# A hybrid DiT block on one core: the first feed-forward's output product in pieces of 2 and a last piece of 4, and the mixer blocks' norm scaling on ScalarE

## The chip, the cores and the metric

The kernel runs on one core of a Trainium2 chip. The metric is the device time of one execution in microseconds, as the median of several runs. The five engines that the profile tells apart are PE (TensorE; its weight loads are listed as PEld), DVE (VectorE), ACT (ScalarE), POOL (GpSimd) and SP (SyncE, which here issues all DMAs).

## The reference, cut to what matters

Only the first feed-forward network (ffn1) and the norm ahead of the mixer are touched. In the reference they are these lines, for the 512 rows of x and, with the same weights, for the 256 rows of the context:

```python
def rmsnorm(x, g):
    y = x32 * lax.rsqrt(jnp.mean(x32 * x32, axis=-1, keepdims=True) + EPS)
    return (y * g.astype(jnp.float32)).astype(x.dtype)

def swiglu(h, w_in, w_out):
    gate, up = jnp.split(h @ w_in, 2, axis=-1)
    return (jax.nn.silu(gate) * up) @ w_out

h = ada_pre(x, norm_pre[l, 0], m[0], m[1])
x = ada_post(x, swiglu(h, ffn1_w_in[l], ffn1_w_out[l]), norm_post[l, 0], m[2], 0.5)
h = ada_pre(x, norm_pre[l, 1], m[3], m[4])
y, yc = mixer(h, hc, ...)
```

`ada_post` is z + w * gate * rmsnorm(y, g); `ada_pre` is rmsnorm(z, g) * (1 + scale) + shift. The model width is 1024 and the inner width of ffn1 2816. After the mixer comes a second feed-forward (ffn2), which the change leaves alone.

## The kernel before, in words

All 768 rows are worked on together as six blocks of 128 rows: four of x (0 to 3) and two of the context (4 and 5), taken in the order 4, 5, 0, 1, 2, 3 (`ORDER`). Every product is made from float32 values split into a high and a low part (`split`, lines 65 and 66: a cast on ACT, then a subtraction on DVE), with three matmuls in place of one (`mm3`, lines 71, 72 and 74; `product`, lines 425 to 427).

The inner width is 22 column tiles of 128. `in_tile(j)` makes one column tile of silu(gate) * up, for all 768 rows. Tiles 0 and 1 are made by the plain product (`std_tile`); meanwhile DVE and ACT form sums of the input blocks (`sums1`, `sums1_t4`), and from tile 2 on a tile is made by a scheme of seven half-size products (`product` seven times, with 12 matmuls in each), for which `weights(j)` loads the gate and the up columns (512 KB each, into the tile `wraw`, of which there are three buffers), splits the up columns (g0), adds them up in place (lines 411 to 414) and splits the results (g2, g1 and the half-size c). The high and low parts go into `wh` and `wl`, of three buffers each. The forms of the input that three of the seven products read stand in `fxh` and `fxl`. The product of form T3 (F_T3), the fifth of the seven, is the last to read `fxl`.

The output product is cut into pieces by `run_pieces`: a piece is a few column tiles whose contributions are summed in PSUM before they are taken out. For a piece, `out_w(j)` loads row block j of the output weights (512 KB, into `wraw` too) and splits it into `woh` and `wol`, of two buffers each in ffn1; the very last block goes into `wh` and `wl`. `out_phase` then runs over the six blocks of rows: six matmuls per column tile and block, two halves of 512 columns. The first piece's sums are copied out by ACT (line 332), those of the middle pieces are added to `tok` by DVE (line 334: twelve additions per piece), and those of the last piece go to `last1`. The pieces of ffn1 are (1, 2, 2, 2, 2, 2, 2, 2, 2, 2, 3). A piece's `out_phase` is written after the first `in_tile` of the next piece, so PE has one `in_tile` between a piece's tiles and its output product.

`last1` works on one block after the last piece's matmuls: the two halves are added (line 727), ACT squares the block and sums it (`rstd`, line 226), POOL makes the reciprocal root in two instructions on 128 values (lines 228 and 229), DVE multiplies by the gate (line 729) and adds the residual (line 730), for which x or the context is loaded again into `wraw` (line 736). Then `pre_xn` makes the norm for the mixer: again squares on ACT, two POOL instructions, and the scaling on DVE (line 234). When two blocks are ready, `make_hT` transposes them on PE (line 250), scales and shifts them on ACT (line 257; the first of eight on DVE, line 255), and splits them on DVE (lines 259 and 260). The mixer's first projections (`proj_tok`, and `part` of its first gate) come next on PE, by pairs of blocks: (4, 5), (0, 1), (2, 3). Their results are copied to `vt` on ACT (line 908).

What sets the order: at the very start of the kernel it is written out by hand (`manual_schedule`); everywhere else the framework orders each engine's instructions when the kernel is built, by the order of the program and the buffers that are free. An engine works through its own list in order, and waits where a value or a buffer is not ready. Parallel to ffn1, DVE computes the modulation vectors in small steps (`background`, lines 637 to 687), 1.7 steps at each `product`.

Of the kernel before, what the change touches and what calls it, by code (L numbers as in the profile page):

```python
# [11 lines left out]
F32R = mybir.dt.float32r  # L12
AF = mybir.ActivationFunctionType
# [3 lines left out]
P = 128  # L17
D = 1024
# [7 lines left out]
NF = FF // P  # L26
# [17 lines left out]
def kernel(ctx: ExitStack, tc: tile.TileContext, i, out):  # L44
    nc = tc.nc
# [5 lines left out]
    def nm(s):  # L51
        uid[0] += 1
        return f"{s}_{uid[0]}"

    def ps(tag="mm", shape=(P, 512)):
        return psum.tile(list(shape), F32, tag=tag, name=nm(tag), bufs=4)

    def ct(shape, tag, dt=F32, bufs=1, pool=None):
        return (pool or core).tile(list(shape), dt, tag=tag, name=nm(tag), bufs=bufs)
# [4 lines left out]
    def split(hi, lo, src):  # L64
        nc.scalar.copy(hi, src)  # L65
        nc.vector.tensor_tensor(out=lo, in0=src, in1=f32(hi), op=ALU.subtract)  # L66

    def mm3(outs, sh, sl, start, stop):

        for o, mh, ml in outs:  # L70
            nc.tensor.matmul(o, lhsT=sh, rhs=mh, start=start, stop=False)  # L71
            nc.tensor.matmul(o, lhsT=sh, rhs=ml, start=False, stop=False)  # L72
        for o, mh, ml in outs:
            nc.tensor.matmul(o, lhsT=sl, rhs=mh, start=False, stop=stop)  # L74

    def steps(work, n):
        while n and work:
            try:
                next(work[0])
                n -= 1  # L80
            except StopIteration:
                work.pop(0)
# [46 lines left out]
    tok = [None] * NT  # L129
# [87 lines left out]
    def rstd(z, n, scratch):  # L217

        ss = ct([P, 1], "ss", bufs=8)
        if isinstance(z, (list, tuple)):  # L220
            s2 = ct([P, 2], "ss2", bufs=4)
            for q, zz in enumerate(z):
                nc.scalar.activation(scratch[:, q * 512:(q + 1) * 512], zz, AF.Square, accum_out=s2[:, q:q + 1])
            nc.vector.tensor_tensor(out=ss, in0=s2[:, 0:1], in1=s2[:, 1:2], op=ALU.add)
        else:
            nc.scalar.activation(scratch, z, AF.Square, accum_out=ss)
        r = ct([P, 1], "rs", bufs=8)
        nc.gpsimd.tensor_scalar(ss, ss, 1.0 / n, EPS, ALU.mult, ALU.add)
        nc.gpsimd.tensor_tensor(out=r, in0=ss, in1=mhalf, op=ALU.pow)
        return r  # L230

    def pre_xn(t, xn):
        r = rstd(tok[t], D, xn)
        nc.vector.tensor_scalar(xn, tok[t], r, None, ALU.mult)
        return xn
# [60 lines left out]
    def tick(n):  # L296

        credit[0] = credit[0] + n if background else 0.0
        while background and credit[0] > 0:
            try:  # L300
                credit[0] -= next(background[0])
            except StopIteration:
                background.pop(0)

    def run_pieces(in_tile, w_out, ntok, pool, pieces, yacc, last, final_pre, order, w4, wo_bufs):
        order = order or range(ntok)

        def out_w(j):
            raw = ct([P, D], "w4", bufs=4, pool=w4) if w4 else ct([P, D], "wraw", bufs=3)
            nc.sync.dma_start(raw, w_out[j * P:(j + 1) * P, :])  # L310
            if j == NF - 1:
                hi, lo = ct([P, D], "wh", F32R, bufs=3), ct([P, D], "wl", F32R, bufs=3)
            else:
                hi = ct([P, D], "woh", F32R, bufs=wo_bufs, pool=pool)
                lo = ct([P, D], "wol", F32R, bufs=wo_bufs, pool=pool)
            split(hi, lo, raw)
            return hi, lo

        def out_phase(acts, ws, first, final):
            for t in order:  # L320
                o = [ps() for _ in range(2)]
                for hs in ((0,), (1,)) if final and t == order[-1] else ((0, 1),):
                    for q, ((ah, al), (wh, wl)) in enumerate(zip(acts, ws)):
                        mm3([(o[h], wh[:, h * 512:(h + 1) * 512], wl[:, h * 512:(h + 1) * 512]) for h in hs],
                            ah[:, t * P:(t + 1) * P], al[:, t * P:(t + 1) * P], q == 0, q == len(ws) - 1)
                if final:
                    last(t, o)
                    continue
                for h in range(2):
                    y = yacc[t][:, h * 512:(h + 1) * 512]  # L330
                    if first:
                        nc.scalar.copy(y, o[h])  # L332
                    else:
                        nc.vector.tensor_tensor(out=y, in0=y, in1=o[h], op=ALU.add)  # L334

        prev = None
        j = 0
        for n, size in enumerate(pieces):
            acts = []
            for q in range(size):  # L340
                acts.append(in_tile(j + q))
                if q == 0 and prev:
                    out_phase(*prev)
            ws = [out_w(j + q) for q in range(size)]
            prev = (acts, ws, n == 0, n == len(pieces) - 1)
            j += size
        tick(1000)
        if final_pre:
            final_pre()
        out_phase(*prev)  # L350
# [10 lines left out]
    class Forms:  # L361
# [28 lines left out]
        def last(self):  # L390
            k = 0
            for z in self.t4:
                n = z.shape[1]
                split(*self.at(F_T4, k, n), z)
                k += n
# [216 lines left out]

    GROUPS = ((0, T), (T, TA))
    HT_STEPS = {5: 8, 1: 8}
    PIECES1 = (1, 2, 2, 2, 2, 2, 2, 2, 2, 2, 3)
    PIECES = (1, 3, 3, 3, 3, 3, 2, 4)
    gg = {}

    with tc.tile_pool(name="f1", bufs=1, reuse_waits="tile") as f1:
# [93 lines left out]
        waiting = {}  # L713
# [4 lines left out]
        def post(t, o, n, v, w4, res):  # L718

            y = tok[t]  # L720
            if not scrs:
                x4 = ct([P, 4, D], "fxh", pool=w4)
                scrs.extend(x4[:, n, :] for n in range(4))
            scr = scrs[t % 4]
            for h in range(2):
                hc = slice(h * 512, (h + 1) * 512)
                nc.vector.tensor_tensor(out=y[:, hc], in0=y[:, hc], in1=o[h], op=ALU.add)
            r = rstd(y, D, ct([P, D], "up", mybir.dt.bfloat16, bufs=2, pool=w4))
            nc.vector.tensor_tensor(out=scr, in0=y, in1=gg[n, v], op=ALU.mult)
            nc.vector.scalar_tensor_tensor(out=y, in0=scr, scalar=r, in1=res, op0=ALU.mult, op1=ALU.add)  # L730
            return scr

        def last1(t, o):
            res = ct([P, D], "wraw", bufs=3)
            src = i["x"][0, t * P:(t + 1) * P, :] if t < NX else i["ctx"][0, (t - NX) * P:(t - NX + 1) * P, :]
            nc.sync.dma_start(res, src)
            scr = post(t, o, 0, 0 if t < NX else 1, f1, res)
            waiting[t] = pre_xn(t, scr)
            for s in sets:
                if t == s[-1]:  # L740
                    if not h2:
                        h2.extend(ct([P, KD, TA], tag, F32R) for tag in ("hh", "hl"))
                    hts.append(make_hT(1, *h2, s, [waiting[q] for q in s], f1, tags=("wch", "wcl")))
            steps(hts, HT_STEPS.get(t, 0))
# [4 lines left out]
        def final_pre():  # L749
            first_w.append(v_w(0))  # L750

        ffn7(i["ffn1_w_in"][0], i["ffn1_w_out"][0], forms1, NT, f1, None, PIECES1, tok, last1, pre=pre1,
             sums=(sums1, sums1_t4), acts=acts1, by_k=True, ticks=1.7, wo_bufs=2, final_pre=final_pre, order=ORDER)
        steps(hts, 1000)
# [13 lines left out]
    with tc.tile_pool(name="mh", bufs=1, reuse_waits="tile") as mh:  # L768
# [180 lines left out]
        for t in range(NX):  # L949
            o = o_tok[t // 2][:, t % 2, :]  # L950
            scr = ct([P, HG], "km", bufs=2, pool=mh)
            r = rstd(o, HG, scr)
# [188 lines left out]
    with tc.tile_pool(name="mg", bufs=1, reuse_waits="tile") as mg:  # L1141
# [44 lines left out]
        with tc.tile_pool(name="yw", bufs=1, reuse_waits="tile", side="right") as yw:  # L1186
            w2 = i["ffn2_w_in"][0]
            wout = []
            for k in range(KD):
                raw = ct([P, D], "wraw", bufs=3)  # L1190
                nc.sync.dma_start(raw, i["w_out"][0, k * P:(k + 1) * P, :])
                hi, lo = ct([P, D], "woh", F32R, bufs=4, pool=yw), ct([P, D], "wol", F32R, bufs=4, pool=yw)
# [35 lines left out]
            for t in range(NX):  # L1228
# [3 lines left out]
                r = rstd(po[t], D, ct([P, D], "junk", mybir.dt.bfloat16, pool=mg))  # L1232
# [86 lines left out]
```

## Time and profile before

| what | value |
| --- | --- |
| time, median of 3 runs | 1470.2 us (1469.75 to 1472.22) |
| the profiled execution's own time | 1468.57 us |
| its span, first to last instruction | 1466.5 us |
| busy in the span: PE, DVE, ACT, POOL | 1398.1, 1154.4, 656.9, 60.9 us |
| mean granted TensorE clock | 0.986 of full speed |

The profile gives for each engine how long it was busy and, for a group of equal instructions, the mean time of one, how long the engine stood idle just before them, and what ended that idle time. A time window can be asked for, in microseconds from the span's start. Matmuls are pipelined: one is listed with its whole passage, and the next begins before it ends, so their pace is read from the starts. ffn1's tiles fill the stretch up to about 543 us; the last piece, `last1` and the mixer's first projections follow.

### The profile page before, as it was taken

The numbers are of one execution on the slowest core, as the hardware profiler recorded it, in microseconds if no ns is written. First come the engines' busy times: TensorE is split into PE (matmuls) and PEld (weight loads), VectorE is DVE, ScalarE is ACT, GpSimd is POOL, SyncE is SP. The second block draws the span as 40 slices with busy tenths as digits, with TensorE's granted clock in tenths as the row PEclk, the third lists the DMA queues.
The fourth block names the chain that finished last, engine by engine and source line by source line (L and its number), as shares of the span: only waits on it lengthen the run. The fifth ranks groups of instructions, "written<-read, shape, count | busy, mean of one in ns | idle before, by whom it ended". The sixth has DMA issues, their size and how long they took to land. (4 is left out here: it accounts for less than half of the span.)

```text
span 1466.5 us, 22992 instructions
## 1 busy us (share of the span) xinstructions
PE 1398.1 (95%) x8864; PEld 1233.1 (84%) x8864; DVE 1154.4 (79%) x2013; ACT 656.9 (45%) x1083; POOL 60.9 (4%) x87
## 2 busy tenths in 40 slices
PE   6899999999999998999999899989898999999997
PEld 3689999999999996889888677767677998999996
DVE  6988888888888868486785789777758887787785
ACT  6553343333333335332335589523247544444442
POOL 3200000000000003000001000000010000000001
PEclk9999999999999999999999899999999999999999
DMA  9333334233333232221212121376534543343211
GB/s 312 100 115 103 113 96 120 87 91 111 90 102 96 80 101 72 83 59 45 60 42 82 41 58 30 113 203 204 170 94 142 163 134 102 99 131 101 87 44 58
DMA packets 195765, 151.61 MB, mean 103 GB/s; under 512 B 8392, under 2 KB 186056, under 8 KB 195656
## 3 DMA queue, kind: packets, MB, share of 16 engines
q1 hardware_dynamic: 195656, 150.15, 33.9%
q8 instruction: 69, 1.13, 0.3%
q14 instruction: 40, 0.33, 0.1%
HBM read 148.02 MB, written 2.10 MB: 102 GB/s over the span
## 5 line engine op out<-in xcount | busy, mean ns | idle before, releaser
L66 DVE TENSOR_TENSOR wl<-wraw,wh 128x1024 fp32r<-128x1024 f32 (+1 forms) x180 | 216.6, 1209 | 78.4 <-ACT wh L65 77.4
L65 ACT CAST wh<-wraw 128x1024 fp32r<-128x1024 f32 (+1 forms) x180 | 184.9, 1031 | 147.2 <-PE aux L426 44.7
L71 PE MATMUL mm<-hh,wh 128*128 128x512 f32 (+2 forms) x488 | 172.1, 356 | 0.3 <-ACT gg L967 0.2
L72 PE MATMUL mm<-hl,wh 128*128 128x512 f32 (+2 forms) x488 | 168.3, 353 | 0.1
L74 PE MATMUL mm<-hh,wl 128*128 128x512 f32 (+2 forms) x488 | 160.4, 359 | 3.4 <-DVE wl L66 3.4
L425 PE MATMUL mm<-hh,wh 128*128 128x256 f32 (+1 forms) x400 | 122.8, 307 | 5.3 <-DVE sg L503 5.1
L425 PE MATMUL aux<-hh,wh 128*128 128x256 f32 (+1 forms) x400 | 121.8, 304 | 2.0 <-ACT wh L65 2.0
L427 PE MATMUL aux<-hh,wl 128*128 128x256 f32 (+1 forms) x400 | 121.6, 304 | 0.0
L427 PE MATMUL mm<-hh,wl 128*128 128x256 f32 (+1 forms) x400 | 121.5, 304 | 0.0
L426 PE MATMUL aux<-hl,wh 128*128 128x256 f32 (+1 forms) x400 | 121.5, 304 | 0.0
L426 PE MATMUL mm<-hl,wh 128*128 128x256 f32 (+1 forms) x400 | 121.4, 304 | 0.0
L71 PEld LDWEIGHTS mm<-hh,wh 128*128 128x128 f32 x488 | 92.8, 191 | 14.4 <-ACT gg L967 0.7
L72 PEld LDWEIGHTS mm<-hl,wh 128*128 128x128 f32 x488 | 93.1, 191 | 10.5 <-DVE hl L557 0.6
L642 DVE SCALAR_TENSOR_TENSOR macc<-wa,cs,macc 128x256 f32<-128x256 f32 x196 | 88.0, 479 | 17.6 <-DMA wa<-w_ada 16.6
L71 PE MATMUL mm<-woh,act 128*128 128x512 f32 x252 | 98.9, 393 | 0.5 <-ACT tok L332 0.4
L74 PEld LDWEIGHTS mm<-hh,wl 128*128 128x128 f32 x488 | 89.1, 192 | 11.1 <-DVE wl L66 3.9
L72 PE MATMUL mm<-wol,act 128*128 128x512 f32 x252 | 98.1, 390 | 0.0
L334 DVE TENSOR_TENSOR tok<-tok,mm 128x512 f32<-128x512 f32 x132 | 84.5, 681 | 15.4 <-PE mm L74 15.4
L425 PEld LDWEIGHTS mm<-hh,wh 128*128 128x128 f32 x400 | 75.9, 190 | 9.1 <-DVE sg L503 7.9
L74 PE MATMUL mm<-woh,act 128*128 128x512 f32 x252 | 78.1, 390 | 0.1
L425 PEld LDWEIGHTS aux<-hh,wh 128*128 128x128 f32 x400 | 75.9, 190 | 2.5 <-ACT wh L65 2.5
L426 PEld LDWEIGHTS mm<-hl,wh 128*128 128x128 f32 x400 | 76.0, 190 | 0.6
(381 smaller groups left out, 3441.5 us busy)
## 6 DMA issues: line engine op xcount, KB each, us to landing
wraw<-ffn_w_in SPq DMA_DIRECT2D x88, 512.0 KB, 4.1
wraw<-mix_w_in SPq DMA_DIRECT2D x42, 512.0 KB, 3.7
wa<-w_ada SPq DMA_DIRECT2D x128, 128.0 KB, 2.1
b7l<-w_ada SPq DMA_DIRECT2D x96, 128.0 KB, 2.6
wraw<-ffn_w_out SPq DMA_DIRECT2D x22, 512.0 KB, 3.7
w<-ffn_w_out SPq DMA_DIRECT2D x22, 512.0 KB, 4.4
wa<-w_ada SPq DMA_DIRECT2D x16, 256.0 KB, 4.1
tok<-w_ada SPq DMA_DIRECT2D x16, 256.0 KB, 5.6
```

The lines of the kernel that those rows point to most:

```text
L65: nc.scalar.copy(hi, src)
L66: nc.vector.tensor_tensor(out=lo, in0=src, in1=f32(hi), op=ALU.subtract)
L71: nc.tensor.matmul(o, lhsT=sh, rhs=mh, start=start, stop=False)
L72: nc.tensor.matmul(o, lhsT=sh, rhs=ml, start=False, stop=False)
L74: nc.tensor.matmul(o, lhsT=sl, rhs=mh, start=False, stop=stop)
L334: nc.vector.tensor_tensor(out=y, in0=y, in1=o[h], op=ALU.add)
L425: nc.tensor.matmul(o, lhsT=wk, rhs=mh, start=first and k == 0, stop=False, skip_group_check=True)
L426: nc.tensor.matmul(o, lhsT=wk, rhs=ml, start=False, stop=False, skip_group_check=True)
L427: nc.tensor.matmul(o, lhsT=wl[:, k0 + k, :], rhs=mh, start=False, stop=k == H4 - 1, skip_group_check=True)
L642: nc.vector.scalar_tensor_tensor(out=a, in0=w, scalar=cs[:, v, k:k + 1], in1=a, op0=ALU.mult, op1=ALU.add)
```

## The change

Three edits. The pieces of ffn1 become nine of 2 tiles and a last one of 4, in place of one of 1, nine of 2 and a last one of 3. The last piece thus has four blocks of output weights at hand; `out_w(20)` is put into a new tile that takes the place of `fxl` (only in ffn1, where `w4` is None). And in `last1` the norm's scaling for the mixer is written as an activation (a copy with a scale per row) on ACT, in place of `pre_xn`, whose last step is on DVE; the squares and the POOL steps stay as they were.

```diff
             raw = ct([P, D], "w4", bufs=4, pool=w4) if w4 else ct([P, D], "wraw", bufs=3)
             nc.sync.dma_start(raw, w_out[j * P:(j + 1) * P, :])
-            if j == NF - 1:
+            if w4 is None and j == NF - 2:
+                x4 = ct([P, 4, D], "fxl", F32R, pool=pool)
+                hi, lo = x4[:, 0, :], x4[:, 1, :]
+            elif j == NF - 1:
                 hi, lo = ct([P, D], "wh", F32R, bufs=3), ct([P, D], "wl", F32R, bufs=3)
...
-    PIECES1 = (1, 2, 2, 2, 2, 2, 2, 2, 2, 2, 3)
+    PIECES1 = (2, 2, 2, 2, 2, 2, 2, 2, 2, 4)
...
             scr = post(t, o, 0, 0 if t < NX else 1, f1, res)
-            waiting[t] = pre_xn(t, scr)
+            r = rstd(tok[t], D, scr)
+            nc.scalar.activation(scr, tok[t], AF.Copy, scale=r)
+            waiting[t] = scr
```

ffn2 has pieces of its own and keeps them, and its norms keep `pre_xn`.

## Rows read from the trace of the kernel before

**Rows 1.** The page's first part: busy time, share of span, instructions.
```profile
PE 1398.1 (95%) x8864; PEld 1233.1 (84%) x8864; DVE 1154.4 (79%) x2013; ACT 656.9 (45%) x1083; POOL 60.9 (4%) x87
```

**Rows 2.** Windows: start:end, length, busy time (instructions) of PE, PEld, DVE, ACT, POOL, clock, DMA.
```profile
76.00:80.00 4.00, 3.49 (x16) 2.30 (x15) 4.00 (x5) 1.49 (x4) 0.00 (x0) 1.00 0.42 124
87.00:94.00 7.00, 7.00 (x30) 5.13 (x30) 6.97 (x12) 6.38 (x11) 0.00 (x0) 1.00 0.47 139
...
100.00:540.00 440.00, 439.02 (x2323) 409.37 (x2323) 374.18 (x634) 159.21 (x235) 0.00 (x0) 1.00 0.33 99
...
543.00:606.00 63.00, 55.25 (x306) 45.35 (x305) 46.90 (x89) 30.61 (x56) 15.81 (x24) 0.95 0.26 82
```

**Rows 3.** Windows, same columns, two short stretches inside the tail.
```profile
585.00:591.00 6.00, 5.18 (x22) 4.08 (x23) 5.68 (x15) 3.07 (x6) 2.82 (x3) 0.73 0.33 95
...
597.00:603.00 6.00, 4.44 (x26) 4.45 (x27) 2.19 (x9) 3.72 (x9) 0.00 (x0) 0.72 0.00 0
```

**Rows 4.** Waits of PE, 543 to 600 us: total, times, longest.
```profile
PE mm L71 <- ACT vt L908: 3.0, 1, 3.0
PE aux L250 <- DVE fxh L234: 2.9, 4, 1.4
```

**Rows 5.** Timeline, PE: start, us, operation; the last piece's first matmuls, its last, `proj_tok` of (2, 3).
```profile
543.21 0.39 PE L71 MATMUL mm<-woh,act 128*128 128x512 f32 x1
...
545.95 0.39 PE L71 MATMUL mm<-woh,act 128*128 128x512 f32 x1
...
573.79 0.39 PE L74 MATMUL mm<-wh,act 128*128 128x512 f32 x1
...
605.65 0.28 PE L71 MATMUL mm<-wh,hh 128*128 128x256 f32 x1
```

**Rows 6.** Groups by line, DVE, 543 to 600 us: busy, mean ns; idle before.
```profile
L727 DVE TENSOR_TENSOR tok<-tok,mm 128x512 f32<-128x512 f32 x12 | 7.9, 681 | 0.8 <-PE mm L74 0.8
L730 DVE SCALAR_TENSOR_TENSOR tok<-fxh,rs,wraw 128x1024 f32<-128x1024 f32 x6 | 7.7, 1283 | 1.6 <-POOL rs L229 1.4
L729 DVE TENSOR_TENSOR fxh<-tok,gg 128x1024 f32<-128x1024 f32 x6 | 7.3, 1221 | 0.1
...
L234 DVE TENSOR_SCALAR fxh<-tok,rs 128x1024 f32<-128x1024 f32 x6 | 4.5, 754 | 3.6 <-POOL rs L229 3.5
```

**Rows 7.** Groups by line, ACT, 543 to 600 us.
```profile
L257 ACT ACTIVATE wcl<-aux,colB,colA 128x256 f32<-128x256 f32 x12 | 6.7, 558 | 4.4 <-PE aux L250 4.2
L226 ACT ACTIVATE fxh<-tok 128x1024 f32<-128x1024 f32 x6 | 6.4, 1061 | 10.1 <-DVE tok L730 10.1
```

**Rows 8.** One line's instructions, L1087 (whole span): ns min/median/max, starts.
```profile
L1087 ACT ACTIVATE s<-s,es x8: 707/730/739, 827.8 to 920.8; 128x512 f32<-128x512 f32 x8
```

**Rows 9.** Timeline of the start, from the lists of DVE, PE and SP.
```profile
75.71 1.22 DVE L66 TENSOR_TENSOR wol<-wraw,woh 128x1024 fp32r<-128x1024 f32 x1
...
76.22 0.76 PE L71 MATMUL mm<-woh,act 128*128 128x512 f32 x2
...
77.00 0.38 SPq L96 DMA_DIRECT2D wraw<-ffn_w_in  x1
...
77.72 2.35 DVE L66 TENSOR_TENSOR wl<-wraw,wh 128x1024 fp32r<-128x1024 f32 x2
...
79.37 0.51 PE L74 MATMUL mm<-hh,wl 128*128 128x384 f32 x2
...
87.00 0.39 PE L72 MATMUL mm<-wol,act 128*128 128x512 f32 x1
...
88.56 1.22 DVE L66 TENSOR_TENSOR wl<-wraw,wh 128x1024 fp32r<-128x1024 f32 x1
...
94.11 0.33 PE L425 MATMUL mm<-hh,wh 128*128 128x384 f32 x1
```

**Rows 10.** Groups by line, DVE, 100 to 540 us: the middle pieces' additions.
```profile
L334 DVE TENSOR_TENSOR tok<-tok,mm 128x512 f32<-128x512 f32 x108 | 69.1, 681 | 10.1 <-PE mm L74 10.1
```

**Rows 11.** DMA issues of the page: count, KB each, median us to landing.
```profile
wraw<-ffn_w_in SPq DMA_DIRECT2D x88, 512.0 KB, 4.1
```

## The prediction

> **What bounds the kernel now.** I read the page's totals first. PE is busy for 1398.1 of 1466.5 us [rows 1], so only work on PE, or a place where PE waits, can set the time. Then the windows [rows 2]: from 100 to 540 us PE is busy for 439.02 of 440 us although DVE is at 374 us. In this stretch a shorter DVE list can give back at most the 1.0 us that PE lacks. The change leaves the number of matmuls as it is, so it must be judged where PE does lack time: the start of ffn1 (0.5 us of 76 to 80) and the tail of ffn1, from the last piece to the mixer's first projections, where PE is busy for 55.25 of 63 us at a mean clock of 0.95.
>
> In the tail the waits [rows 4] name two causes: the transposes wait 2.9 us for the scaling of line 234 on DVE, and the projections 3.0 us for the copy of line 908 on ACT, which frees their PSUM buffer. The rest of the 7.75 us lies in small gaps at `make_hT`. After gaps the granted clock is down: 0.73 and 0.72 in two stretches of 6 us [rows 3], a mix of the two levels, 1.2 and 2.4 GHz. The same busy time at 2.4 GHz would be 5.18 x 0.27 = 1.4 and 4.44 x 0.28 = 1.2 us shorter. So the tail holds 7.75 + 2.6 = 10.4 us that are not work; that is its ceiling.
>
> **The change, part by part.**
>
> *One middle addition round less.* The pieces go from eleven to ten, so line 334 runs twelve times less, each 681 ns [rows 10]: 8.2 us off DVE. They all lay beside a PE that was full [rows 2], so they are worth between 0 and 1.0 us. I take 0.4.
>
> *The last piece has 4 tiles.* For each block of rows PE has 6 more matmuls in the last piece. Their pace is 12 from 543.21 to 545.95 [rows 5], 0.228 us each; 36 of them are 8.2 us that leave the full stretch before 543 us and enter the tail. There they either fill gaps or lengthen it. Who paces the tail? Per block of rows PE has 18 x 0.228 = 4.1 us before, and 5.5 us after. DVE has lines 727, 729, 730 and 234: 7.9 + 7.3 + 7.7 + 4.5 = 27.4 us for six [rows 6], 4.6 us per block, and the splits of `make_hT` come on top. So before, DVE falls behind PE with every block, and PE meets that backlog as waits. Four tiles per block slow PE to about DVE's pace.
>
> *The scaling on ACT.* It takes six instructions of 0.754 us from DVE, and with them DVE's 3.5 us of standing for POOL's reciprocal root [rows 6]: 4.5 + 3.5 = 8.0 us off the list that falls behind. ACT is busy for only 30.6 of the 63 us [rows 2]. The new instruction's price isn't in the trace. Its nearest rows are the square of the same shape, 1.061 us [rows 7], and the same operation with a scale per row at half the length, 0.730 us [rows 8], so 1.06 to 1.46 us. I take 1.15, nearer to the row of the same shape. Each block's own chain gets 0.4 us longer, DVE's list 0.75 us shorter.
>
> This instruction is where the Trainium skill speaks against the change. ScalarE: Activation LUTs, section Rules for kernel authors, says to give add and mul to VectorE and not ScalarE. The rows agree that one such instruction is faster there. If each block's chain set the tail, as this rule fears, the six would cost 6 x 0.4 = 2.4 us, and my sum below would shrink from -4.1 to -1.7 us.
>
> *What the tail gives.* Its bounds are a loss of 2.4 us (six longer chains, nothing filled) and a gain of 10.4 us (no gap, full clock). By its terms: the wait for the scaling goes from 2.9 to 1.5 us, as ACT takes it up sooner but each engine's list still holds the order of the build; the wait for the `vt` copy is halved, 3.0 to 1.5 us, because with 8.2 us more of PE work ahead of the projections the activations of the last `make_hT` are nearer their end; the small gaps go from 1.85 to 1.15 us; the clock loses 1.0 instead of 2.6 us. Together 5.2 us. The last two blocks' hT isn't late next: it is needed at 605.65 us [rows 5], and the last piece's matmuls end at 573.79 us, so PE has some 30 us of other blocks' products to do meanwhile.
>
> *The start.* The first piece has two tiles, so its output product comes after tile 2 and no longer between tiles 1 and 2. Before, it does two services [rows 9]. From 76.22 us its first matmuls fill the time in which PE lacks the low part of tile 1's up columns (the two splits at 77.72 us; the first product with it starts at 79.37). From 87.0 to 94.1 us the rest of it runs while DVE prepares tile 2. DVE has no slack in either stretch: 4.00 of 4 us and 6.97 of 7 [rows 2]. Now the first service: the first of the two splits ends at about 78.9 us; without the `wol` split at 75.71 ahead of it, some 1.1 us on the list, the low part is there at about 77.8, so PE stands from 76.2 to 77.8, 1.6 us, against 0.5 before. The second: tile 1 ends at 77.8 + 7.6 = 85.4 us, its 7.6 us being 79.37 to 87.0. Tile 2's first two products are 24 matmuls of 384 columns, at 0.228 x 384 / 512 us each [rows 5] some 4.2 us, so the g2 split is needed at 89.6 us; before, it is done at 88.56 + 1.22 = 89.8. With DVE's order otherwise kept that is 0.2 us late. I add another 0.2 for the second low part behind it. Sum of the start: 1.1 + 0.4 = +1.5 us. Its bounds: -0.5 us (no gap left) and +8.2 us (the 36 matmuls of cover gone and DVE no earlier).
>
> *The fourth weight block in the place of `fxl`.* It must wait for the fifth product of tile 21, which ends two products, about 4.2 us, before the last piece can start. Its split costs DVE 1.22 us [rows 9] and ACT about what a square of that shape takes, 1.06 us [rows 7]; PE wants it after two tiles of the first block, 12 matmuls or 2.7 us later [rows 5]. Cost nothing; the cover is 4.2 + 2.7 us against some 2.3. If other splits come ahead of it, up to 1 us. The longer hold of one load buffer delays the reload of x (line 736), which is wanted only at line 730, behind the first block's matmuls, square and root.
>
> **Sum**: -0.4 - 5.2 + 1.5 = -4.1 us. Against the profiled execution's own 1468.57 us that is 1464.5; the median of the runs stands 1.6 us higher, so 1470.2 - 4.1 = **1466.1 us**.
>
> **The rivals.**
>
> *Forecast* (0.52): the tail's gaps fill, the start costs little. Own range: tail 2.5 to 9.5, start 0 to 3.5, which allows for one being good where the other is poor: 1461.5 to 1467.3.
>
> *No difference, the start takes it* (0.22). There are three load buffers. Now w0, w1 and tile 1's up columns hold them, and tile 2's gate columns can be loaded only after a `wol` split has freed one. If DVE does that split only after tile 2's first low part, at about 84 us in place of 77, where the load is issued now [rows 9], the columns land 4.1 us later [rows 11], at 89; four additions of 128x512 (0.68 us each, as in [rows 10]), a cast and a split (2.3 us) follow, and g2 is there at 94 and not 89.6. The start then costs 1.1 + 4.5 = 5.6 us: -0.4 - 5.2 + 5.6 = 0, 1470.2 us. For it: DVE's full windows. Against it: the first `wol` split stood early in DVE's list before.
>
> *No difference, the tail stays* (0.10). The edit doesn't do what it says: DVE's time wasn't what PE waited for, but the order fixed at the build, with transposes put ahead of products that were ready. Then the tail gives only the 1.5 us of half the `vt` wait, and 1470.2 - 0.4 - 1.5 + 1.5 = 1469.8 us. For it: PE stood still while its next products had their operands. Against it: DVE's list is dense in the tail, 46.9 of 63 us, most of it in the middle.
>
> *Slower, ACT becomes the tail's list* (0.16). The scaling now stands in ACT's list, where it waits for POOL, and with it the activations of `make_hT` and the `vt` copies that come behind it; or it stands behind a group of seven activations of line 257, 7 x 0.56 = 3.9 us [rows 7]. That happens for the second and the third pair of blocks, 7.8 us, and the tail goes from -5.2 to +2.6: 1470.2 - 0.4 + 2.6 + 1.5 = 1473.9 us. It decides once ACT holds the scalings back by more than 5 us more than DVE did. For it: ACT already waits in this stretch for one lane after another (10.1 us for line 730 [rows 7]). Against it: half of ACT's time is free. The rule of the Trainium skill named above (ScalarE: Activation LUTs, Rules for kernel authors) has this mechanism's sign; the time given here comes from the rows alone.
>
> **How the numbers follow.** A measurement here tells about 0.2%, 2.9 us, from no change. The forecast is faster than that (0.52), the two middle cases are the same (0.32), the last is slower (0.16). The range goes from the forecast's good end, 1461.5, to 1473.0 us, just short of the slower case; it leaves out about 1 in 10 on either side.
>
> **What would show it.** Line 334 with twelve fewer additions and 100 to 540 us still without gaps; the last piece starting some 8 us earlier, less what the start lost; PE's idle time in the tail falling from 7.75 to about 4 us with no wait of 3 us for line 908; a gap of 1 to 2 us where tile 1 waits for its low part. The scaling on ACT at 1.1 to 1.2 us. The forecast is wrong if PE stands for more than 4 us between tiles 1 and 2, if the transposes wait longer for ACT than they did for DVE, or if the clock in the tail stays low after gaps that stayed.

## The result and the profile after

The changed kernel takes 1459.9 us (median of 4 runs, 1459.8 to 1462.2) where the kernel before takes 1470.3 us in the same comparison: a ratio of 0.9938, 95% interval 0.9921 to 0.9956. A second sample gave 0.9941 (0.9921 to 0.9961). So it is faster by 0.6%: some 9 us by the ratios, 10 us by the medians. The forecast had the direction and the place, but gave 4.1 us, and the time lies 1.6 us below the end of its range.

The two profiled executions lie closer together than the medians: spans of 1466.5 and 1460.4 us. Executions of one kernel differ by some us here (the kernel before ran from 1465.0 to 1474.6 us in 23 runs), so in one pair of traces only stretches of some length are compared below, and differences of a few us between kernels are taken from the timed runs.

The page's totals of after come first; they answer to [rows 1]. DVE is 10.2 us lighter, ACT 6.9 us heavier; the number of PE's instructions is the same.

```profile
PE 1394.3 (95%) x8864; PEld 1233.6 (84%) x8864; DVE 1144.2 (78%) x1995; ACT 663.8 (45%) x1089; POOL 57.6 (4%) x87
```

Windows of after, with the columns of [rows 2]. The first two are the start, the third the middle, the fourth the tail (from the last piece to the first 128x512 product of the mixer), the last the one stretch of the tail with a low clock, which answers to [rows 3].

```profile
76.00:80.00 4.00, 3.39 (x20) 3.07 (x19) 4.00 (x5) 1.11 (x3) 0.00 (x0) 1.00 0.06 19
...
87.00:94.00 7.00, 6.91 (x37) 6.20 (x36) 7.00 (x12) 4.16 (x5) 0.00 (x0) 1.00 0.06 20
100.00:535.00 435.00, 433.55 (x2300) 405.19 (x2300) 367.35 (x623) 166.35 (x246) 0.00 (x0) 1.00 0.34 99
535.30:609.70 74.40, 68.46 (x411) 58.73 (x410) 45.75 (x85) 39.96 (x66) 11.57 (x24) 0.98 0.24 75
571.00:577.00 6.00, 3.71 (x15) 2.92 (x15) 3.22 (x7) 3.20 (x5) 1.83 (x4) 0.73 0.21 63
```

The same tail, between the same two matmuls, in the windows of before:

```profile
543.00:614.30 71.30, 63.55 (x376) 53.65 (x375) 49.35 (x91) 33.34 (x60) 15.81 (x24) 0.95 0.24 74
```

The reader is to see three things. PE is in the tail 71.3 us before and 74.4 after: with 36 more matmuls, 8.2 us of work at the pace of [rows 5], the tail grew by only 3.1, so it gave 5.1 us. PE's idle time in it went from 71.30 - 63.55 = 7.75 to 74.40 - 68.46 = 5.94 us. And the mean clock rose from 0.95 to 0.98: counted on PE's busy time, as the forecast counted it, 63.55 x 0.05 = 3.2 us of full speed were missing, and 68.46 x 0.02 = 1.4 are now. These two account for an estimated 1.8 + 1.8 of the 5.1 us; the other 1.5 can't be assigned in these windows, whose clock is given in hundredths.

The waits of after in 535 to 600 us (total, times, longest), which answer to [rows 4]. The wait for the `vt` copy, 3.0 us before, is gone from PE's list. The transposes now wait 5.8 us for the scaling, twice what they waited before, and it is the only wait that PE's list still has; none is for the fourth block of output weights.

```profile
ACT fxh L226 <- DVE tok L733: 8.4, 5, 2.3
...
PE aux L250 <- ACT fxh L742: 5.8, 5, 2.3
ACT fxh L742 <- POOL rs L229: 5.7, 5, 2.0
...
DVE tok L733 <- POOL rs L229: 4.6, 4, 2.0
DVE tok L730 <- PE mm L74: 4.5, 5, 1.6
```

Groups by line of after, in the tail (the last one: DVE, 92 to 532 us). They answer to [rows 6, 7, 10]. Lines 730, 732 and 733 are the former 727, 729 and 730; line 742 is the new scaling, 337 the middle pieces' additions.

```profile
L730 DVE TENSOR_TENSOR tok<-tok,mm 128x512 f32<-128x512 f32 x12 | 7.8, 683 | 4.5 <-PE mm L74 4.5
L733 DVE SCALAR_TENSOR_TENSOR tok<-fxh,rs,wraw 128x1024 f32<-128x1024 f32 x6 | 7.7, 1282 | 4.6 <-POOL rs L229 4.6
...
L742 ACT ACTIVATE fxh<-tok,rs 128x1024 f32<-128x1024 f32 x6 | 6.9, 1150 | 5.8 <-POOL rs L229 5.7
...
L337 DVE TENSOR_TENSOR tok<-tok,mm 128x512 f32<-128x512 f32 x96 | 61.5, 682 | 8.1 <-PE mm L74 7.9
```

The scaling takes 1.150 us on ACT. Before, DVE's first addition in `last1` hardly waited for PE (0.8 us in [rows 6]); now it waits 4.5 us. DVE no longer runs behind PE in the tail of this kernel.

The timeline of after, from the lists of DVE and PE. It answers to [rows 5, 9].

```profile
77.02 1.22 DVE L66 TENSOR_TENSOR wl<-wraw,wh 128x1024 fp32r<-128x1024 f32 x1
...
78.29 0.61 PE L74 MATMUL mm<-hh,wl 128*128 128x384 f32 x2 [0.61 <-DVE wl L66]
...
79.02 2.35 DVE L66 TENSOR_TENSOR wol<-wraw,woh 128x1024 fp32r<-128x1024 f32 x2
...
90.21 0.39 PE L71 MATMUL mm<-woh,act 128*128 128x512 f32 x1
...
91.64 2.35 DVE L66 TENSOR_TENSOR wl<-wraw,wh 128x1024 fp32r<-128x1024 f32 x2
...
535.49 0.39 PE L71 MATMUL mm<-woh,act 128*128 128x512 f32 x1
...
609.71 0.40 PE L71 MATMUL mm<-hh,wh 128*128 128x512 f32 x1
```

At the start PE stands 0.61 us for tile 1's low part. The low part is split first, at 77.02, and both `wol` splits come behind it. The g2 split of tile 2 comes later than in before (91.64, where [rows 9] have 88.56), but PE doesn't stand for it: from 90.21 us it does matmuls of the first piece's own output product.

The last piece starts at 535.49 us, 7.7 us before the 543.21 of [rows 5]. In the two traces that keep the old start and have a last piece of 4 (last4_dve and last4_act, below) it starts at 534.39 and 535.60 us. So the 8.2 us of matmuls cost about their length in the stretch that they left.

### The profile page after: what moved, and what is told of

Read it like the earlier page. It is cut to its first block, busy times and chain, and to the rows that moved or that the text cites. A ratio compares the mean times of both kernels' runs of the same rounds, so it can differ in the third digit from the quotient of the medians.

```text
span 1460.4 us, 22968 instructions
## 1 busy us (share of the span) xinstructions
PE 1394.3 (95%) x8864; PEld 1233.6 (84%) x8864; DVE 1144.2 (78%) x1995; ACT 663.8 (45%) x1089; POOL 57.6 (4%) x87
## 5 line engine op out<-in xcount | busy, mean ns | idle before, releaser
L66 DVE TENSOR_TENSOR wl<-wraw,wh 128x1024 fp32r<-128x1024 f32 (+1 forms) x180 | 216.8, 1210 | 78.3 <-ACT wh L65 77.1
L74 PEld LDWEIGHTS mm<-hh,wl 128*128 128x128 f32 x488 | 88.6, 191 | 12.3 <-DVE wl L66 5.0
L71 PE MATMUL mm<-woh,act 128*128 128x512 f32 x240 | 94.1, 392 | 0.0
L72 PE MATMUL mm<-wol,act 128*128 128x512 f32 x240 | 93.9, 391 | 0.0
L337 DVE TENSOR_TENSOR tok<-tok,mm 128x512 f32<-128x512 f32 x120 | 76.9, 682 | 12.7 <-PE mm L74 12.5
L430 PEld LDWEIGHTS mm<-hh,wl 128*128 128x128 f32 x400 | 76.0, 190 | 0.0
```

The lines of the kernel that those rows point to most:

```text
L430: nc.tensor.matmul(o, lhsT=wl[:, k0 + k, :], rhs=mh, start=False, stop=k == H4 - 1, skip_group_check=True)
```

## The experiments

Twelve runs, each compared with the kernel before on the same chip. "Tail" is the time from the last piece's start to the mixer's first 128x512 product in the run's trace; "net" is the tail less 8.2 us for every 36 matmuls added to it.

| run | last piece, scaling | ratio to before (95%) | tail | net | PE idle | clock |
| --- | --- | --- | --- | --- | --- | --- |
| before | 3, DVE | 1 | 71.3 | 71.3 | 7.75 | 0.95 |
| start_only | 3, DVE | 0.9996 (0.9983 to 1.0008) | 72.2 | 72.2 | 8.35 | 0.95 |
| act_only | 3, ACT | 0.9964 (0.9951 to 0.9976) | 69.4 | 69.4 | 6.77 | 0.95 |
| pieces_only | 4, DVE | 0.9940 (0.9923 to 0.9957) | 73.4 | 65.2 | 5.84 | 1.00 |
| last4_dve | 4, DVE | 0.9951 (0.9935 to 0.9966) | 74.0 | 65.8 | 6.24 | 1.00 |
| after_again | 4, ACT | 0.9941 (0.9921 to 0.9961) | 74.4 | 66.2 | 5.97 | 0.98 |
| last4_act | 4, ACT | 0.9953 (0.9940 to 0.9966) | 73.6 | 65.4 | 6.27 | 1.00 |
| more_dve | 4, ACT | 0.9947 (0.9930 to 0.9963) | 73.6 | 65.4 | 6.29 | 1.00 |
| later_ht | 4, ACT | 0.9960 (0.9944 to 0.9975) | 77.1 | 68.9 | 7.90 | 0.96 |
| pad_before | 3 and dummies, DVE | 1.0008 (0.9996 to 1.0019) | 73.4 | 65.2 | 5.77 | 1.00 |
| alt_scale | 4, both | 0.9934 (0.9919 to 0.9949) | 72.1 | 63.9 | 5.08 | 1.00 |
| last5_act | 5, ACT | 0.9929 (0.9913 to 0.9944) | 80.3 | 63.9 | 5.13 | 1.00 |
| last5_dve | 5, DVE | 0.9942 (0.9927 to 0.9956) | 80.0 | 63.6 | 4.68 | 1.00 |

### The change again, and its three parts apart

**after_again** has no edit; it is the changed kernel beside the others on their chip.

> The changed kernel once more, to measure the gain with more rounds. The two profiles differ by 6.1 us of span, the medians by 10.3 us. If the profiled executions are as good as any, the ratio comes out near 0.9958; if the medians are, near 0.993. All theories expect the same here; it says how large the thing to be explained is.

Measured: 1458.6 us against 1469.2, ratio 0.9941.

**pieces_only** has the new pieces and leaves the scaling on DVE:

```diff
-            r = rstd(tok[t], D, scr)
-            nc.scalar.activation(scr, tok[t], AF.Copy, scale=r)
-            waiting[t] = scr
+            waiting[t] = pre_xn(t, scr)
```

> The new pieces (nine of 2, one of 4) with the scaling left on DVE. Theory A (the tail is paced by DVE's backlog; both edits relieve it, the 8.2 us of matmuls by filling gaps and the scaling by shortening the list): about 60% of the whole gain, 4 to 6 us. Rival B (the scaling on ACT is what matters, the pieces only move work): under 1.5 us. Rival C (the start is where the gain is, since the first piece's PSUM copies no longer hold PE): nearly all of the gain.

Measured: 1460.0 us, ratio 0.9940, 8.8 us below before: the whole of the change's gain without its second part. Theory A had asked for 4 to 6 us and missed. Rival C had asked for this number, but put it down to the start, which start_only below excludes. PE's waits in 535 to 600 us are these:

```profile
PE aux L250 <- DVE fxh L234: 3.2, 4, 1.3
PE mm L71 <- ACT vt L911: 1.6, 1, 1.6
```

The window of the tail of pieces_only, with the columns of [rows 2]:

```profile
535.20:608.60 73.40, 67.56 (x410) 57.37 (x410) 49.77 (x91) 33.51 (x60) 10.57 (x24) 1.00 0.24 76
```

With more PE work the wait for `vt` is halved, 3.0 to 1.6 us, the forecast's term for it, and the mean clock of the tail is 1.00, its upper level, 2.4 GHz. The wait for the scaling isn't shorter than before (3.2 against 2.9 us), and DVE's groups by line in 535 to 600 us show that DVE still hardly waits for PE:

```profile
L730 DVE TENSOR_TENSOR tok<-tok,mm 128x512 f32<-128x512 f32 x12 | 8.0, 683 | 1.4 <-PE mm L74 1.3
...
L234 DVE TENSOR_SCALAR fxh<-tok,rs 128x1024 f32<-128x1024 f32 x6 | 4.5, 753 | 5.3 <-POOL rs L229 5.3
```

So four tiles per block did not bring the scaling to PE in time, as theory A and the forecast had it; they filled other gaps and kept the clock up.

**act_only** is the kernel before, its old pieces kept, with the scaling on ACT:

```diff
-            waiting[t] = pre_xn(t, scr)
+            r = rstd(tok[t], D, scr)
+            nc.scalar.activation(scr, tok[t], AF.Copy, scale=r)
+            waiting[t] = scr
```

> The old pieces with the scaling on ACT. Theory A: 2 to 4 us faster than before. Rival B: nearly all of the gain. Rival D (the scaling's place matters only once PE is slowed to DVE's pace by a last piece of 4): within 1 us of before.

Measured: 1464.2 us, ratio 0.9964, 5.3 us below before. PE's waits in 541 to 606 us are these:

```profile
PE mm L71 <- ACT vt L910: 2.8, 1, 2.8
...
PE aux L250 <- ACT fxh L739: 1.6, 3, 1.2
```

The window of the tail of act_only:

```profile
541.90:611.30 69.40, 62.63 (x375) 54.13 (x375) 45.83 (x85) 39.64 (x66) 11.05 (x24) 0.95 0.25 76
```

Alone, the move does what the forecast said of it: the transposes' wait for the scaling falls from 2.9 to 1.6 us, the tail is 1.9 us shorter. The wait for `vt` and the clock are as before. Rival D (no effect without four tiles) is excluded; theory A had asked for 2 to 4 us. The rest of the 5.3 us isn't in the tail of this one trace, and the timed interval (3.5 to 7.2 us) doesn't reach down to 1.9. In the trace 1.1 us more lie ahead of the tail and 3.0 behind it, where the kernel is unchanged: from the tail's end to the last instruction the traces of before, after and the twelve runs take 847.8 to 853.1 us, without any order by the last piece. So where the rest of the 5.3 us comes from stays open.

The two parts don't add up: 5.3 and 8.8 us alone, 8.7 together. The waits don't show one lag that either part takes away: alone, the move shortens the wait for the scaling and leaves `vt` and the clock, and the pieces do the reverse. With both, the wait for the scaling is 5.8 us, so what the move gave alone is lost again; why is not shown. Once the last piece has four tiles, the scaling's place makes no difference that can be measured (0.9941 and 0.9940; in the next group 0.9953 and 0.9951).

**start_only** is the kernel before with pieces that begin with 2, as many of them as before, and a last one of 3:

```diff
-    PIECES1 = (1, 2, 2, 2, 2, 2, 2, 2, 2, 2, 3)
+    PIECES1 = (2, 2, 2, 2, 2, 2, 2, 2, 2, 1, 3)
```

> Pieces of nine times 2, then 1 and 3, scaling on DVE: the new start, the old last piece, and the old number of eleven pieces. Theory A, as forecast: 1.5 us slower than before. By the changed kernel's profile, whose start lost nothing (PE gaps of 0.6 and 0.1 us where 0.5 stood before): within 1 us of before. Rival C: 4 us or more faster.

Measured: 0.9996, that is -0.6 us (-2.5 to +1.2). The first output product after tile 2 costs nothing that shows, and rival C, a gain of 4 us or more by the start, falls. Its trace has the same short wait at the start as the changed kernel's:

```profile
78.64 0.62 PE L74 MATMUL mm<-hh,wl 128*128 128x384 f32 x2 [0.62 <-DVE wl L66]
```

### Last piece without the new start, and one round of additions back

**last4_dve** and **last4_act** keep the first piece of 1 and all eleven pieces, and have a last piece of 4; one scales on DVE, the other on ACT:

```diff
-    PIECES1 = (2, 2, 2, 2, 2, 2, 2, 2, 2, 4)
+    PIECES1 = (1, 2, 2, 2, 2, 2, 2, 2, 2, 1, 4)
```

> Pieces of 1, eight times 2, 1 and 4, scaling on DVE: the old start and the old number of eleven pieces with the new last piece. Theory A: as fast as the new pieces with the scaling on DVE, within 1.5 us of it, since start and count are worth little. Rival C (start) and rival E (the twelve DVE additions that fall away in the middle): no faster than before by more than 1.5 us.

> The same pieces, 1, eight times 2, 1 and 4, with the scaling on ACT: the changed kernel but for its start and its count of pieces. Theory A: within 1.5 us of the changed kernel. Rivals C and E: slower than the changed kernel by 3 us or more.

Measured: 1459.3 and 1460.0 us against 1467.2, ratios 0.9951 and 0.9953. The last piece alone gives about 7 us. By the ratios the two are 1.6 and 1.8 us behind the same kernels with the new start and one round less, a little more than the 1.5 us that theory A allowed; the intervals (2 to 3 us on either side) can't tell that from nothing. Rivals C and E, by which last4_dve would gain no more than 1.5 us, fall.

**more_dve** is the changed kernel with pieces (2, 2, 2, 2, 2, 2, 2, 2, 1, 1, 4), which puts the twelve additions back on DVE.

> The changed kernel with one more piece in the middle (eight times 2, then 1, 1 and 4): twelve additions of 0.68 us, 8.2 us, back on DVE, start and last piece as in the changed kernel. Theory A: within 1 us of the changed kernel, since PE was full in the middle with them too. Rival E: 3 us or more slower than the changed kernel.

Measured: 0.9947, within the intervals of the kernels with one round less. The 8.2 us of DVE time in the middle are worth nothing that shows, where the forecast had 0.4 us.

**later_ht** is the changed kernel with the steps of `make_hT` one block of rows later:

```diff
-    HT_STEPS = {5: 8, 1: 8}
+    HT_STEPS = {0: 8, 2: 8}
```

In this run the first pair's scaled rows are partly written over before they are transposed: block 0's rows go to the place of block 4's. So the mixer works on other values, and the first pair's transposes wait for block 0 too; the amount of work is the same.

> The changed kernel with the transposes of the first and the second pair of blocks placed one block later in the program (after blocks 0 and 2 in place of 5 and 1). In the changed kernel PE still stands 5.8 us for the scaling on ACT ahead of the transposes. If PE's fixed order puts them too early, 2 to 4 us of that goes and the kernel beats both; if what is late is the chain of the last pair, within 1 us of the changed kernel, or slower because the later transposes then hold up the projections.

Measured: 0.9960, 0.1 to 0.3% above the other kernels with a last piece of 4, at the edge of what the intervals tell. PE's waits in 536 to 606 us:

```profile
PE aux L250 <- ACT fxh L742: 6.1, 3, 4.3
```

The timeline, from the lists of ACT and PE, shows what the longest of these waits is for:

```profile
562.84 1.15 ACT L742 ACTIVATE fxh<-tok,rs 128x1024 f32<-128x1024 f32 x1 [0.94 <-POOL rs L229]
...
564.04 2.40 PE L250 MATMUL aux<-ident,fxh 128*128 128x128 f32 x10 [4.31 <-ACT fxh L742]
```

This is the third scaling of the tail, block 0's: the first pair waits 4.3 us for rows that aren't its own. After this gap the clock is down (0.50 from 564 to 567 us), and it is 0.96 over the tail. In all the tail is 2.7 us longer than the changed kernel's, net. The other two waits are 0.3 and 1.5 us, in sum 1.8 us against the changed kernel's 5.8. So the run does not tell what a later place of the transposes is worth; none of its expected outcomes is settled by it.

### Work put into the tail for its own sake

**pad_before** is the kernel before with 36 matmuls in the last piece that do nothing: the real sum starts over them.

```diff
+                    for q in range(3) if final and ntok == NT else ():
+                        for h in hs:
+                            nc.tensor.matmul(o[h], lhsT=acts[0][0][:, t * P:(t + 1) * P],
+                                             rhs=ws[0][0][:, h * 512:(h + 1) * 512], start=True, stop=True)
                     for q, ((ah, al), (wh, wl)) in enumerate(zip(acts, ws)):
```

> The kernel before, with 36 more matmuls of 128x512 in the last piece: each block's first column tile is multiplied three more times into both halves, and the real sum then starts over them. The output is unchanged; it is work that does nothing. At the pace of the last piece, 0.228 us each, it is 8.2 us of PE. Theory G (the tail has room: PE's stretch from the last piece to the mixer's first products is set by DVE's list and by the granted clock, and work put into its gaps also keeps the clock up): the tail grows by 2 to 3.5 us, as it does where real work is moved there (3.1 us in the changed kernel's profile, 2.2 with the scaling left on DVE), low-clock stretches fall from two to one or none, and the time is 1 to 3.5 us above the kernel before, ratio 1.0007 to 1.0024. Theory H (PE work in the tail costs its full length, and the gain of the longer last piece came from the stretch it left): 8.2 us above, ratio 1.0056, in the time and in the tail.

Measured: 1470.0 us against 1469.1, ratio 1.0008 (0.9996 to 1.0019), so +1.1 us (-0.6 to +2.8). The dummies are this group by line of PE in 535 to 606 us:

```profile
L325 PE MATMUL mm<-woh,act 128*128 128x512 f32 x36 | 9.7, 395 | 0.0
```

PE's waits of pad_before in 543 to 606 us:

```profile
PE aux L250 <- DVE fxh L234: 3.2, 4, 1.4
...
PE mm L71 <- ACT vt L912: 1.6, 1, 1.6
```

The window of the tail of pad_before:

```profile
543.00:617.00 74.00, 68.23 (x415) 57.97 (x414) 50.36 (x91) 33.52 (x60) 10.56 (x24) 1.00 0.23 71
```

This is the run that decides. 8.2 us of useless PE work cost about 1.1 us: theory H, by which they cost their length, asked for a ratio of 1.0056 and falls. In the trace the tail grew by 2.1 us, so it took in 6.1 of them, and what paid for them shows: the clock 1.00 in place of 0.95 (3.2 us by the working above) and the idle time 5.77 in place of 7.75 us (2.0). The waits are those of pieces_only within 0.1 us. So what the longer last piece does in the tail is this: it moves 8.2 us of matmuls out of a stretch where they cost their full length into one where they cost about 1.1, which gives 7.1 us (5.4 to 8.8 by the interval).

### Looking for more

**last5_act** and **last5_dve** have a last piece of 5, with the blocks of output weights and the last tile's activations in further places of `fxl` and `wh`:

```diff
-    PIECES1 = (2, 2, 2, 2, 2, 2, 2, 2, 2, 4)
+    PIECES1 = (2, 2, 2, 2, 2, 2, 2, 2, 1, 5)
...
-            if w4 is None and j == NF - 2:
-                x4 = ct([P, 4, D], "fxl", F32R, pool=pool)
-                hi, lo = x4[:, 0, :], x4[:, 1, :]
-            elif j == NF - 1:
+            if w4 is None and j == NF - 3:
+                hi, lo = x4s[0][:, 0, :], x4s[0][:, 1, :]
+            elif j == NF - 1 or w4 is None and j == NF - 2:
...
+            if slot[0] == NF:
+                x4s.append(ct([P, 4, D], "fxl", F32R, pool=f1))
+                return [x4s[0][:, n, :TA] for n in (2, 3)]
```

> The changed kernel with pieces eight of 2, one of 1 and a last one of 5: 36 more matmuls, 8.2 us, leave the full stretch for the tail; scaling on ACT. In the changed kernel the tail still has 5.9 us of idle PE and 1.7 us of lost clock. Theory G: some of it fills, the tail grows by 4 to 7.5 of the 8.2 us, so 1 to 4 us below the changed kernel, ratio to before 0.9915 to 0.9935. Theory I (what idle time is left in the tail does not come from PE running ahead; it is the length of a block pair's own chain over ACT, POOL and the transposes, which PE work does not fill): within 1 us of the changed kernel, ratio 0.9935 to 0.995, with the transposes' waits for ACT still over 5 us.

> The same with the scaling on DVE. With 22.5 matmuls' worth of time per block more than in the kernel before PE needs 6.8 us per block of rows, against some 5.3 of DVE with the split additions, so DVE has no backlog left and its scaling comes in time. Theory G: as the one with ACT or up to 1.5 us better, because each block's chain is 0.4 us shorter and the copies of vt are not behind scalings; ratio 0.991 to 0.9935. Theory I: 0.9935 to 0.995.

Measured: 0.9929 and 0.9942. (A fifth tile means 12 matmuls more per block than in before, 30 against 18; the 22.5 of the expectation is a slip, its 6.8 us per block is right.) In the trace with ACT the 8.2 us cost 80.3 - 74.4 = 5.9 us of tail, so there is little room left. The window of this tail is:

```profile
528.80:609.10 80.30, 75.17 (x446) 64.20 (x445) 46.64 (x86) 40.86 (x67) 12.90 (x24) 1.00 0.25 77
```

PE's waits for the scaling in 535 to 600 us of last5_act:

```profile
PE aux L250 <- ACT fxh L746: 4.9, 5, 1.5
```

PE still stands for 4.9 us in five waits for the scaling, with 72 matmuls more in its tail than before. The fourth tile's 8.2 us had lengthened the tail by 3.1, the fifth's by 5.9: such work fills the tail less and less. That the rest is a pair's own chain of squares, POOL and scaling, as theory I has it, fits but isn't shown. Whether the fifth tile gives 1 or 2 us isn't settled; theory G had asked for a ratio of 0.9935 or less of both and got it of one, and theory I for waits of over 5 us.

**alt_scale** scales blocks 5, 1 and 3 on DVE and the others on ACT:

```diff
+            if t in (5, 1, 3):
+                waiting[t] = pre_xn(t, scr)
+            else:
                 r = rstd(tok[t], D, scr)
```

> The changed kernel with the scaling of every second block (5, 1 and 3) back on DVE. Theory G, with both engines' lists of use: the transposes' wait for a scaling falls from 5.8 us to about 4, and the time is 1 to 2 us below the changed kernel. Theory J (with four tiles in the last piece it is all the same which engine scales, since neither list is behind): within 1 us of the changed kernel and of the version that leaves all scaling on DVE, ratio 0.9935 to 0.995.

Measured: 0.9934. PE's waits in 535 to 600 us are these:

```profile
PE aux L250 <- DVE fxh L234: 2.5, 3, 1.1
PE aux L250 <- ACT fxh L745: 1.8, 2, 1.3
```

The window of the tail of alt_scale:

```profile
535.10:607.20 72.10, 67.02 (x411) 57.44 (x410) 47.29 (x88) 36.47 (x63) 11.49 (x24) 1.00 0.25 79
```

The wait for the scaling falls to 4.3 us, as expected, and the tail is 2.3 us shorter than the changed kernel's, but the timed ratio can't be told from the changed kernel's (0.9941, interval to 0.9921), so neither theory is settled. No version here beats the changed kernel by more than the measurement tells.

## Why the prediction was wrong in size

**What bounds the kernel: right.** The middle was full and stayed full (433.55 of 435 us), the rounds of additions (108 to 96) are worth nothing that shows, and the tail is where the matmuls found room.

**The start, +1.5 us: this step failed.** By start_only it is -0.6 us (-2.5 to +1.2). The forecast let the low part of tile 1 come at 77.8 us on an otherwise unchanged PE order, with PE standing 1.6 us, and took the first piece's 36 matmuls as gone from the stretch of tile 2. What the trace shows is that PE's order was remade when the kernel was built: it does the high-part products first and stands 0.61 us, and some of the first piece's output matmuls go between tile 2's products just where g2 is late (90.21 us). The cover was moved, not lost, and the step is worth nothing that shows. The rival in which the start takes everything has the same fault: g2 did come later than before, but PE had other work to do.

**The tail, -5.2 us: this term was mis-sized.** In the one pair of traces the tail gave 5.1 us, as if the forecast were exact, but that is luck, since its terms were not so. The step that failed is the one from four tiles and a shorter DVE list to shorter waits for the scaling; what took the matmuls in was the clock that came back, the wait for `vt` and the small gaps.

- The wait for the scaling: 2.9 to 1.5 us forecast, 5.8 measured with both parts, 3.2 with the pieces alone. The scaling on ACT costs what was said (1.150 us against 1.15), but ACT now stands 5.7 us for POOL in front of it. The forecast gave DVE 3.5 us of its standing for POOL back; there DVE stands 4.6 us at line 733 in place of 1.4 at the old line 730, so together 4.9 us before and 4.6 now, and almost nothing came back.
- The wait for `vt`: 3.0 to 1.5 us forecast, 1.6 with the pieces alone, none with both parts.
- The clock: 2.6 to 1.0 us forecast, a gain of 1.6; some 3.2 to 1.4 in the changed kernel's trace, and a mean of 1.00 in six of the eight other traces with a last piece of 4 or its weight in dummies. The two stretches of [rows 3] held most of the loss, but the forecast let 1.0 us of it stand without a reason; where none stands, this term alone is worth some 3 us.
- The small gaps: 1.85 to 1.15 us forecast. PE's idle time of 5.94 less the wait of 5.8 leaves about 0.1.

In the timed runs the longer last piece is worth more than the tail gave in that pair: 7.1 us by pad_before, about 7 by last4_dve, 8.8 by pieces_only. That is nearer to the ceiling of 10.4 us, which the forecast had halved. The traces taken together say the same. The tail ends at 614.3 and 616.2 us with the old last piece and scaling (before, start_only), and at 606.9 to 609.7 in the seven traces with a last piece of 4 other than later_ht (613.1). That is 4.6 to 9.3 us earlier, and the pair of before and after stands at the low end of it.

The clock of the timed executions fits this, though no run sets it apart as a cause. Its mean is 0.9853, 0.9858 and 0.9852 in the three larger samples of before, 0.9858 in act_only, 0.9861 in start_only, 0.9875 to 0.9892 in all kernels with a last piece of 4 other than later_ht (0.9862), and 0.9879 in pad_before, which has the dummies and no shorter time. From one execution to the next it goes with the time only in part: six of the changed kernel have spans of 1456.2 us at 0.990 and 0.991, 1459.4 at 0.987, 1462.5 at 0.984, but the first four have 1458.0 at 0.986 and 1460.4 at 0.987. Both traces of the changed kernel are of the longest execution in their sample.

**A sign that came true in a faster kernel.** The forecast was to be wrong if the transposes waited longer for ACT than they had for DVE. They do, 5.8 against 2.9 us. It shows that the forecast's term for this wait was wrong, and yet the kernel is faster, since PE's idle time in the tail fell in sum, from 7.75 to 5.94 us. The Trainium skill's rule (ScalarE: Activation LUTs, Rules for kernel authors), to give add and mul to VectorE, has the single instruction right, 1.150 against 0.754 us. It speaks of the single instruction and not of a chain; that reading, and the sum of -1.7 us, are the forecast's own. This sum is further off than -4.1, and act_only shows the opposite sign: the move alone makes this kernel 5.3 us faster, although the instruction itself is 0.4 us longer. In this tail VectorE is the busier engine, 49.4 against 33.3 us in the window of before.

**The rivals.** ACT's list as the new bound needed 5 us more of holding back than DVE's; it was 2.9, and PE waited for no `vt` copy. That the tail stays is refuted by pad_before: it gave way as soon as PE had other work. How much of the 5.8 us that PE still waits is due to the order fixed at the build isn't shown: later_ht, where the first pair waits for another block's rows, can't tell it.

With the steps as measured, nothing at the start and -7.1 to -8.8 us for the longer last piece, the sum is 1461.4 to 1463.1 us from the median of 1470.2. By the larger sample's ratio the result is 0.9941 x 1470.2 = 1461.5 us, the very end of the range; by the first medians it is below it.

## What to carry to other kernels

Where PE waits for other engines in a stretch, ask what a matmul costs there: independent PE work moved into it from a full stretch may be nearly free, as 8.2 us for 1.1 were here. Two edits to the same stretch are not to be added up without a run of each: here 5.3 and 8.8 us gave 8.7 together. When a waiting engine is filled, count the clock that comes back with the gaps as a term of its own, and give a reason for whatever part of its loss is to stay.

## What the runs showed of the hardware that was not expected

Executions of one and the same program differ in the mean granted clock by more than the change does: six executions of the changed kernel have 0.984 to 0.991, with 6.3 us between the spans, where the samples of before and of the changed kernel differ by 0.003 in their means.

POOL's instruction on 128 values (line 228) takes 690 ns on average in the tail of before and 372 in the changed kernel; here is the group by line in the tail of before:

```profile
L228 POOL TENSOR_SCALAR ss<-ss 128x1 f32<-128x1 f32 x12 | 8.3, 690 | 521.8 <-ACT up L226 500.3 <-ACT fxh L226 18.8 <-DVE hh L259 2.6
```

And the same group in the tail of the changed kernel:

```profile
L228 POOL TENSOR_SCALAR ss<-ss 128x1 f32<-128x1 f32 x12 | 4.5, 372 | 521.0 <-ACT up L226 502.4 <-ACT fxh L226 18.6
```

It is shorter with the scaling on either engine (322 ns in pieces_only and pad_before, 349 in act_only; at most 476, in last5_dve) and long in start_only (758), which has the old last piece and the scaling on DVE. That is 8.3 - 4.5 = 3.8 us in twelve instructions of the blocks' chains, for which the forecast had no term; how much of it reached PE isn't shown. Single ones go from 0.19 to 2.06 us, the longest of them in before:

```profile
588.67 2.06 POOL L228 TENSOR_SCALAR ss<-ss 128x1 f32<-128x1 f32 x1 [3.10 <-ACT fxh L226]
```

In the traces of before, start_only, pad_before, act_only and after, each of these instructions that takes more than 0.3 us lies beside DVE instructions whose operands are all in SBUF (lines 66, 234, 259, 260 and the product with the gate), and ends within 0.1 us of the end of one of them; the one above ends at 590.73, DVE's last split at 590.68. Where DVE stands, or does an addition from PSUM (line 727), they take about 0.19 us. So a DVE that is always at work goes with a longer way over POOL for each block in these traces. No run varies this alone.
